# Moving the value differences of a stick-breaking attention into the projection stage, and tying five groups of splits and scans behind others, in a hybrid block on one Trainium2 core

## The chip, the cores and the metric

The kernel runs on one core of one Trainium2 chip. The metric is the device time of one execution in microseconds; lower is better. The times of the kernel before are 2502.95, 2505.12 and 2508.58 us, so the median is 2505.12 us. The profile shown comes from one further execution of the same program.

Engines are named as in the profile: PE (TensorE, matmuls and transposes), PEld (its weight loads), ACT (ScalarE), DVE (VectorE), POOL (GpSimd) and SP (SyncE, which issues the transfers).

## What is computed

One layer of a decoder trunk on 1024 positions of width 1024, all in float32. The part that the change touches is the first sub-layer, token mixing:

```
h = rms_norm(x)
q, k, v, z, xbc, dt_raw, ga, gs = split(h @ w_in)
o_att = stick_breaking_attention(q, k, v)          # 16 heads of 64
o_ssm = ssd_branch(z, xbc, dt_raw, ...)            # Mamba-2, 32 heads in 4 groups
merged = sigmoid(ga) * (o_att @ w_br_att) + sigmoid(gs) * (o_ssm @ w_br_ssm)
x = x + rms_norm(merged @ w_mix_out)
...                                                # then cross-attention and SwiGLU

# one attention head, query t, key s < t:
#   beta[t,s] = sigmoid(q_t . k_s / 8)
#   A[t,s]    = beta[t,s] * prod_{s<j<t} (1 - beta[t,j]),   o_t = sum_s A[t,s] v_s
```

The kernel does not form A. With n[t,j] = sigmoid(-q_t . k_j / 8) = 1 - beta[t,j] and the suffix product N[t,s] = prod_{s<=j<t} n[t,j], A[t,s] = N[t,s+1] - N[t,s]. Summed by parts, the output is a sum of N[t,s] - 1 times the difference of two neighbouring rows of v. These differences, one tile of 128 x 8 x 64 per head, are the "differences of values" of the change.

## The kernel before

Every float32 operand of a matmul is split into a rounded high part and a low part that holds the rest, and a product is three matmuls (high by high, low by high, high by low). `hi_sb` (L110 on) makes a high part, on ACT (L119) or POOL (L115); `lo_of` (L121) makes the low part, by default on DVE (L122). Names that end in h or "hi" are high parts, in l or "lo" low parts.

The stages that matter here, in order of time:

- **First stage, to about 58 us:** norm of x, its transposes in split form, the first products for v.
- **Second stage, about 58 to 270 us:** `rest_of_v` (L494 on) forms the remaining values as five products t1, t2, b22, t3, t4, and stores rows of v to `v_d`; `token_major` (L591 on) forms z in the same way, twice, with seven products each (b11, t2, b21, t1, t3, b22, t4). A `product` (L477) makes four pairs of splits zh and zl (L482, L483: from zr or other tiles, five buffers of each), one for each of four k, and then runs 48 matmuls (L490 to L492); the splits of the next product run beside the matmuls of the present one. In `rest_of_v` the operands t3 and t4 are read back from `tc_d` in eight loads of 256 KB (zk) and split as well (L512, L513).
- **Convolutions and gates, about 270 to 645 us.**
- **Attention, about 645 to 1086 us:** heads in eight pairs. For a pair of heads, projections of q and k are made from loaded weights (wraw, split into whi and wlo) by matmuls mm (L125 to L127). `ev_q` copies the result to qs (ACT, L852 and L853), forms its low part gt (DVE, L854), and moves halves with transfers (L845); `ev_k` does the same for kh and kl (L861 to L863). `scores` (L896) makes for a head and a block b of 128 queries the scores sc (L908, L909), their sigmoid n (ACT, L910) and its suffix product by a scan on DVE (L911) of (b + 1) x 128 elements a row: block 6 has 896, blocks 0 to 3 belong to half 0 of a head and 4 to 7 to half 1. `values` (L916) transposes N by blocks of 128 keys (tr, L925), splits N - 1 into wth (ACT, L928) and wtl (DVE, L929), and sums av with two matmuls per key block (L937, L938), three steps behind the transposes. The last three key blocks of a half are 384, 256 and 128 wide. `interleave` (L955) puts the value steps of one half, the scores of the next half and the projections of the pair after next into one order.
- Before, `differences` (L881) runs in attention: at each even head it loads two shifted copies va and vb of two heads' values from `v_d` (512 KB each, one buffer each), POOL subtracts them (L888, 128x1024), and for each head POOL makes the high and the low part of v (L115, L122).
- **SSD stage from 1086 us:** `open_four` (L1088) loads cfm, btm and others for four chunks and splits them into ch, cl, bh and bl; before, nothing ties these splits to the attention stage. A table load for the exponential is tied behind the last sigmoid of the scores (L990, L996, L997), while the last gates' sigmoids (L875) come later and are not counted in it.

The order on each engine is set by a scheduler at build time from the written order, the dependences and estimated times; each engine then executes its instructions strictly in that order, and SP issues its transfers in order too, so that a transfer that waits for its buffer holds up those behind it. `behind` (L217) adds a tie: the instructions made inside it are put after the named ones on their engine.

## Time and profile before

| | |
|---|---|
| median of 3 runs | 2505.12 us |
| the profiled execution | 2511.1 us, of which the span is 2509.4 us |
| mean granted clock of PE | 0.995 |
| second stage | 58 to 270 us |
| attention | 645 to 1086 us, eight pairs at some 50 us each |
| length of one product of the second stage | 10.9 us (48 matmuls) |

How to read the rows in the prediction. A row of a time line has the start in us, the duration in us (of a run of like instructions when "x4" stands at its end, first start to last end), the engine, the line, the operation, its output and inputs by the program's names, and in brackets how long the engine stood idle just before it and what released it. A row of the list of waits has the engine and what waited, what it waited for, and then the total, the number of times and the longest. A row of the windows has the stretch and its length, then the busy time of PE, PEld, DVE, ACT and POOL with the number of instructions that started in it, the granted clock of PE, the busy share of the transfer engines and GB/s. A row of a group has the count after "x", and behind the bar the busy time in us, the mean of one in ns, and the idle time before.

### The profile page before, as it was taken

What the parts mean: (1) busy time and instruction counts of PE and PEld (TensorE: products, weight loads), DVE (VectorE), ACT (ScalarE), POOL (GpSimd) and SP (SyncE); (2) the same over time, 40 slices, a digit from 0 to 9 for tenths busy, and PEclk for the clock granted to TensorE, in tenths of its full rate; (3) what the DMA queues carried; (4) which work ended last, traced back from release to release, by engine and by line L of the source; (5) the groups of instructions that cost most, each with busy time, mean ns of one, the idle gap of its engine ahead of it and who ended that gap; (6) DMA issues with size and microseconds to landing.
All of it is one profiled execution on the core that took longest, in us unless ns stands there. A gap on an engine that the chain in (4) does not pass through costs nothing. (4 is left out here: it accounts for less than half of the span.)

```text
span 2509.4 us, 33330 instructions
## 1 busy us (share of the span) xinstructions
PE 2447.4 (98%) x12306; PEld 2015.2 (80%) x12306; DVE 1806.5 (72%) x2237; ACT 1165.5 (46%) x2058; POOL 657.3 (26%) x545
## 2 busy tenths in 40 slices
PE   7999999999999999989999999999999999999998
PEld 5788888888778888877877778888888888888887
DVE  7665877776587888689898774487468655666997
ACT  5333455555465666466644312344435333344433
POOL 3221545443211111134444141102012332220001
PEclk9999999999999999999999999999999999999999
DMA  7431443333534343366332481331241322334322
GB/s 249 157 118 47 141 139 113 104 106 93 156 101 110 89 122 89 89 191 207 108 110 77 129 275 59 120 116 51 84 151 63 103 79 76 95 97 164 131 101 101
DMA packets 249132, 295.62 MB, mean 118 GB/s; under 512 B 17023, under 2 KB 169096, under 8 KB 248842
## 3 DMA queue, kind: packets, MB, share of 16 engines
q1 hardware_dynamic: 248682, 292.45, 37.0%
q8 instruction: 97, 1.59, 0.3%
q10 hardware_dynamic: 288, 1.05, 0.1%
q14 instruction: 65, 0.53, 0.1%
HBM read 202.20 MB, written 74.45 MB: 110 GB/s over the span
## 5 line engine op out<-in xcount | busy, mean ns | idle before, releaser
L911 DVE TENSOR_TENSOR_SCAN n<-n,mask 128x128 f32<-128x128 f32 (+7 forms) x128 | 190.0, 1511 | 24.5 <-ACT n L910 21.2
L122 DVE TENSOR_TENSOR sw<-sf,sw 128x512 fp32r<-128x512 f32 x142 | 126.9, 897 | 72.0 <-ACT sw L119 69.9
L119 ACT ACTIVATE sw<-sf 128x512 fp32r<-128x512 f32 x142 | 88.9, 628 | 155.8 <-PE mm L230 139.1
L928 ACT ACTIVATE wth<-tr,mone 128x512 fp32r<-128x512 f32 x192 | 110.7, 585 | 83.3 <-PE tr L925 81.3
L929 DVE SCALAR_TENSOR_TENSOR wtl<-tr,wth 128x512 fp32r<-128x512 f32 x192 | 99.7, 544 | 48.3 <-ACT wth L928 48.3
L693 DVE SCALAR_TENSOR_TENSOR b<-b,prmT,b 128x1023 f32<-128x1023 f32 (+2 forms) x72 | 109.6, 1522 | 16.9 <-ACT b L687 16.3
L122 DVE TENSOR_TENSOR sw<-wr,sw 128x512 fp32r<-128x512 f32 x107 | 99.2, 929 | 23.9 <-ACT sw L119 23.8
L196 POOL TENSOR_TENSOR sf<-wr,wr 128x512 f32<-128x512 f32 x36 | 53.2, 1477 | 229.8 <-DMA wr<-in_w_gu_dram 82.3
L229 PE MATMUL mm<-h,sw 128*128 128x512 f32 x288 | 112.0, 389 | 0.0
L230 PE MATMUL mm<-h,sw 128*128 128x512 f32 x288 | 111.7, 389 | 0.0
L910 ACT ACTIVATE n<-sc 128x512 f32<-128x512 f32 (+1 forms) x192 | 88.6, 494 | 46.6 <-PE tr L925 28.7
L228 PE MATMUL mm<-h,sw 128*128 128x512 f32 x288 | 109.9, 389 | 0.0
L125 PE MATMUL mm<-oth,bw 128*128 128x512 f32 x256 | 104.5, 408 | 3.9 <-DVE a L1259 2.3
L173 POOL TENSOR_SCALAR rstd<-ms 128x1 f32<-128x1 f32 x74 | 26.9, 363 | 307.8 <-ACT x L180 228.3
L127 PE MATMUL mm<-oth,bw 128*128 128x512 f32 x256 | 101.3, 396 | 0.0
L126 PE MATMUL mm<-otl,bw 128*128 128x512 f32 x256 | 101.1, 395 | 0.0
L127 PE MATMUL p<-bw,h 128*128 128x512 f32 x256 | 100.1, 392 | 0.5 <-DVE h L122 0.5
L126 PE MATMUL p<-bw,h 128*128 128x512 f32 x256 | 99.9, 390 | 0.0
L125 PE MATMUL p<-bw,h 128*128 128x512 f32 x256 | 99.7, 390 | 0.0
L925 PE MATMUL tr<-ident,n 128*128 128x128 f32 x576 | 95.4, 274 | 4.0 <-DVE wtl L929 4.0
L115 POOL TENSOR_SCALAR v<-va 128x512 fp32r<-128x512 f32 x16 | 20.6, 1289 | 286.8 <-PE av L938 165.9
L119 ACT ACTIVATE zh<-zr 128x512 fp32r<-128x512 f32 x72 | 45.0, 631 | 104.7 <-PE ma L492 52.3
(664 smaller groups left out, 7753.9 us busy)
## 6 DMA issues: line engine op xcount, KB each, us to landing
wr<-in_w_in_dram SPq DMA_DIRECT2D x36, 512.0 KB
wr<-in_w_gu_dram SPq DMA_DIRECT2D x72, 256.0 KB
zr<-in_w_in_dram SPq DMA_DIRECT2D x28, 512.0 KB
wraw<-in_w_in_dram SPq DMA_DIRECT2D x20, 512.0 KB
gu_d<-t SPq DMA_DIRECT2D x36, 256.0 KB
zs_d<-zo SPq DMA_DIRECT2D x32, 256.0 KB
xs_d<-b SPq DMA_DIRECT2D x32, 256.0 KB
kl<-gt SPq DMA_DIRECT2D x64, 128.0 KB
```

The costliest lines, as they stand in the source:

```text
L119: A.activation(o, i, AF.Copy)
L122: eng.tensor_tensor(o, i, hi.bitcast(F32), ALU.subtract)
L125: first = T.matmul(ps, sh, mh, start=start, stop=False)
L126: T.matmul(ps, sh, ml, start=False, stop=False)
L127: T.matmul(ps, sl, mh, start=False, stop=stop)
L228: T.matmul(ps, w[0][:, k, :], bh, start=first and k == 0, stop=False, skip_group_check=True)
L229: T.matmul(ps, w[0][:, k, :], bl, start=False, stop=False, skip_group_check=True)
L230: ins = T.matmul(ps, w[1][:, k, :], bh, start=False, stop=last and k == 3, skip_group_check=True)
L693: V.scalar_tensor_tensor(acc[:, sh:], y[:, :S - sh], cw(3 - sh, f), acc[:, sh:], ALU.mult, ALU.add)
L911: V.tensor_tensor_scan(nt[:, 0:L][:, ::-1], nt[:, 0:L][:, ::-1], mask[:, S - L:][:, ::-1], 1.0, ALU.mult, ALU.max)
L928: A.activation(wh[:, t0 * P:], pt[:, t0 * P:], AF.Identity, bias=mone)
L929: V.scalar_tensor_tensor(wl[:, t0 * P:], pt[:, t0 * P:], -1.0, wh[:, t0 * P:].bitcast(F32), ALU.add, ALU.subtract)
```

## The change

Five things are changed.

1. In `rest_of_v` the high parts of t3 and t4 are tied behind the last high part of product t2, and the low parts behind its last low part.
2. The differences of values are made in `token_major`: `value_pair` loads va and vb for a pair of heads, `differences` subtracts them on DVE behind the last low part of a product, splits the result on ACT and DVE and stores both heads' tiles to a new scratch `dv_d`. Eight products of the fourteen carry one pair each. In attention, `values_of` only loads a head's finished tile (512 KB, 4 KB a row).
3. The scan of block 6 is tied behind the 256-wide low part of half 0 of the same head.
4. The tie of the exponential's table load (now L1025) covers the gates' sigmoids.
5. `open_four`'s high parts are tied behind the last wth of attention and its low parts behind the last wtl.

The diff, cut:

```diff
                 pa_ = bank("ma")
+                for e in (V, A):
+                    e.on = True
                 product(pa_, a11, "t2", True, True)
+                lasts = [e.last for e in (A, V)]
...
                         nc.sync.dma_start(t, src[:, k, :])
-                        hi_sb(hb[nm][0][:, k, :], t, "a")
-                        lo_of(hb[nm][1][:, k, :], t, hb[nm][0][:, k, :])
+                        with behind(lasts[:1]):
+                            hi_sb(hb[nm][0][:, k, :], t, "a")
+                        with behind(lasts[1:]):
+                            lo_of(hb[nm][1][:, k, :], t, hb[nm][0][:, k, :])
...
+            def value_pair(hp):
+                va, vb = [mk(dvp, [P, NCH, P], F32, n) for n in ("va", "vb")]
+                for t, r in ((va, 0), (vb, 1)):
+                    nc.sync.dma_start(t, v_d[r:S + r, hp * P:(hp + 1) * P].rearrange("(c p) d -> p c d", p=P))
+                loaded.append((hp, va, vb))
+
+            def differences(after):
+                hp, va, vb = loaded.pop()
+                with behind([after]):
+                    V.tensor_tensor(va, va, vb, ALU.subtract)
+                for j in range(2):
+                    dv = va[:, :, j * HD:(j + 1) * HD]
+                    vt = mk(dvp, [P, NCH, P], F32R, "v", 2)
+                    hi_sb(vt[:, :, 0:HD], dv, "a")
+                    lo_of(vt[:, :, HD:P], dv, vt[:, :, 0:HD])
+                    nc.sync.dma_start(dv_d[2 * hp + j], vt.bitcast(F32).rearrange("p c d -> p (c d)"))
+                if hp + 1 < NH // 2:
+                    value_pair(hp + 1)
...
-                product(pa_, a12, "b21", False, True)
+                low = product(pa_, a12, "b21", False, True)
+                if not loaded and j == 1:
+                    value_pair(0)
+                else:
+                    differences(low)
...
-                product(pb_, s1, "t1", True, False)
+                differences(product(pb_, s1, "t1", True, False))
...
-                product(pa_, s3, "t3", True, False)
+                differences(product(pa_, s3, "t3", True, False))
...
+                if loaded:
+                    differences(low)
...
-                    A.activation(gt, ps, AF.Sigmoid)
+                    sig.append(A.activation(gt, ps, AF.Sigmoid))
...
-            def differences(h):
-
-                j = h % 2
-                if j == 0:
-                    va, vb = [mk(vp, [P, NCH, P], F32, n, bufs=1) for n in ("va", "vb")]
...
-                    G.tensor_tensor(va, va, vb, ALU.subtract)
-                    dvs[0] = va
...
-                hi_sb(vt[:, :, 0:HD], dv, "p")
-                lo_of(vt[:, :, HD:P], dv, vt[:, :, 0:HD], G)
-                heads[h]["v"] = vt
+            def values_of(h):
+
+                vt = heads[h]["v"] = mk(vp, [P, NCH, P], F32R, "v")
+                nc.sync.dma_start(vt.bitcast(F32).rearrange("p c d -> p (c d)"), dv_d[h])
...
-                    V.tensor_tensor_scan(nt[:, 0:L][:, ::-1], nt[:, 0:L][:, ::-1], mask[:, S - L:][:, ::-1], 1.0, ALU.mult, ALU.max)
+                    with behind([lows[h, 0, 2]] if b == 6 else []):
+                        V.tensor_tensor_scan(nt[:, 0:L][:, ::-1], nt[:, 0:L][:, ::-1], mask[:, S - L:][:, ::-1], 1.0, ALU.mult, ALU.max)
...
-            sig_last = sig[-1:]
+            sig_last, high_last, low_last = sig[-1:], highs[-1:], [lows[NH - 1, 1, 2 * 4 - 1]]
...
-            hi_sb(bh, btm, "a")
-            lo_of(bl, btm, bh)
...
-            hi_sb(ch, cfm, "a")
-            lo_of(cl, cfm, ch)
+            with behind(high_last):
+                hi_sb(bh, btm, "a")
+                hi_sb(ch, cfm, "a")
+            with behind(low_last):
+                lo_of(bl, btm, bh)
+                lo_of(cl, cfm, ch)
```

In the rows of order that follow, a row has the line, the operation, output and inputs with their buffer numbers, and the shape. Line numbers of the changed kernel differ from those of the kernel before.

**ACT in `rest_of_v`**, around 72 us of the profile. zh are the splits of product t2 (source zr), t3h and t4h those of the operands that are read back. Before:

```order
L119 ACTIVATE t3h_649<-zk_830 128x512
L119 ACTIVATE t4h_651<-zk_834 128x512
L119 ACTIVATE t4h_651<-zk_838 128x512
L119 ACTIVATE t4h_651<-zk_842 128x512
L119 ACTIVATE zh_756<-zr_629 128x512
L119 ACTIVATE zh_760<-zr_631 128x512
```

And in the changed kernel:

```order
L49 ACTIVATE zh_760<-zr_630 128x512
L49 ACTIVATE zh_764<-zr_632 128x512
L49 ACTIVATE zh_768<-zr_632 128x512
L120 ACTIVATE t3h_650<-zk_822 128x512
L120 ACTIVATE t3h_650<-zk_826 128x512
```

The three splits of t2's product now stand ahead of all eight of t3 and t4; before, the first of them stood behind seven.

**DVE in an odd head of attention**, around 696 us of the profile. A row with "mask" is a scan and its last number is the length; wtl are low parts of the weights N - 1. Before:

```order
L929 SCALAR_TENSOR_TENSOR wtl_5711<-tr_5706,wth_5710 128x384
L911 SCALAR_TENSOR_TENSOR n_987_5809<-n_987_5809,mask_5276 128x768
L911 SCALAR_TENSOR_TENSOR n_993_5829<-n_993_5829,mask_5276 128x896
L929 SCALAR_TENSOR_TENSOR wtl_5723<-tr_5719,wth_5722 128x256
L929 SCALAR_TENSOR_TENSOR wtl_5737<-tr_5734,wth_5736 128x128
L911 SCALAR_TENSOR_TENSOR n_1000_5854<-n_1000_5854,mask_5276 128x1024
```

And in the changed kernel, from the same low part on:

```order
L939 SCALAR_TENSOR_TENSOR n_1017_5911<-n_1017_5911,mask_5385 128x768
L957 SCALAR_TENSOR_TENSOR wtl_5825<-tr_5821,wth_5824 128x256
L957 SCALAR_TENSOR_TENSOR wtl_5839<-tr_5836,wth_5838 128x128
L939 SCALAR_TENSOR_TENSOR n_1030_5956<-n_1030_5956,mask_5385 128x1024
L939 SCALAR_TENSOR_TENSOR n_1042_6012<-n_1042_6012,mask_5385 128x128
L957 SCALAR_TENSOR_TENSOR wtl_5887<-tr_5881,wth_5886 128x512
L957 SCALAR_TENSOR_TENSOR wtl_5908<-tr_5903,wth_5907 128x384
L123 TENSOR_TENSOR wlo_6264<-wraw_6261,whi_6263 128x1024
L902 TENSOR_TENSOR gt_5985<-mm_5877,kh_5857 128x512
L939 SCALAR_TENSOR_TENSOR n_1051_6040<-n_1051_6040,mask_5385 128x256
L939 SCALAR_TENSOR_TENSOR n_1060_6075<-n_1060_6075,mask_5385 128x384
L957 SCALAR_TENSOR_TENSOR wtl_5928<-tr_5924,wth_5927 128x256
L939 SCALAR_TENSOR_TENSOR n_1023_5931<-n_1023_5931,mask_5385 128x896
```

The 896-wide scan has left its place ahead of the 256-wide low part (wtl_5723 before, wtl_5825 now) and stands behind the next 256-wide one, eleven instructions later. On PE the transposes of its tile follow: in odd heads three matmuls mm, in even heads six, now stand between the transposes of blocks 4 and 5 and that of block 6, which before followed one another.

**ACT at the start of attention**, around 646 us of the profile. b are copies of the last convolution's transposes, qs those of the first projection of q. Before:

```order
L681 ACTIVATE b_861_5215<-tr_5210 128x512
L852 ACTIVATE qs_5312<-mm_5287 128x512
L853 ACTIVATE qs_5313<-mm_5287 64x512
L119 ACTIVATE whi_5433<-wraw_5431 128x1024
L852 ACTIVATE qs_5312<-mm_5320 128x512
```

And in the changed kernel:

```order
L720 ACTIVATE b_893_5324<-tr_5319 128x512
L120 ACTIVATE whi_5542<-wraw_5540 128x1024
L891 ACTIVATE qs_5421<-mm_5396 128x512
L892 ACTIVATE qs_5422<-mm_5396 64x512
L891 ACTIVATE qs_5421<-mm_5429 128x512
```

The split of the next weights, whi, now stands ahead of both copies of the first half; on DVE wlo likewise stands ahead of gt.

More of the change, by code (lines that the diff above doesn't have):

```diff
@@ L88, in hybrid_block @@
     g_d = scr("g_d", [2 * D, S])
+    dv_d = scr("dv_d", [NH, P, S])
     o_d = [scr(f"o_d{i}", [D, S]) for i in range(2)]
@@ L121, in lo_of @@
     def lo_of(o, i, hi, eng=V):
-        eng.tensor_tensor(o, i, hi.bitcast(F32), ALU.subtract)
+        return eng.tensor_tensor(o, i, hi.bitcast(F32), ALU.subtract)
     def mm3(ps, sh, sl, mh, ml, start, stop):
@@ L456, in hybrid_block @@
             cup = pool(p1, "cumul")
+            dvp = pool(p1, "dv", 1, side="right")
             psp = pool(p1, "psz", 4, PSUM)
@@ L482, in product @@
                     hi_sb(ws[k][0], ts[k // 2][:, k % 2, :], "a")
-                    lo_of(ws[k][1], ts[k // 2][:, k % 2, :], ws[k][0])
+                    low = lo_of(ws[k][1], ts[k // 2][:, k % 2, :], ws[k][0])
                 kc = [(k, c) for k in range(4) for c in range(4)]
@@ L492, in product @@
                     T.matmul(ps[c], bl[:, k, cs], wh, start=False, stop=last and k == 3, skip_group_check=True)
+                return low
             def rest_of_v():
@@ L505, in rest_of_v @@
                 pa_ = bank("ma")
+                for e in (V, A):
+                    e.on = True
                 product(pa_, a11, "t2", True, True)
+                lasts = [e.last for e in (A, V)]
+                for e in (V, A):
+                    e.on, e.last = False, None
                 both(lambda q: V.tensor_tensor(a12[q], a12[q], a11[q], ALU.subtract))
@@ L534, in rest_of_v @@
                     store_v(c, 1, u[c])
+            def value_pair(hp):
[15 more added lines that the diff above has]
+                    value_pair(hp + 1)
+            loaded = []
             def dt_chain(load):
@@ L629, in token_major @@
                     V.tensor_tensor(w[c], u[c], pb_[c], ALU.add)
-                product(pb_, s4, "b22", False, True)
+                low = product(pb_, s4, "b22", False, True)
+                if loaded:
+                    differences(low)
                 for c in range(4):
@@ L633, in token_major @@
                     put(c + 4, i0 + 1, w[c])
-                product(pa_, a22, "t4", False, True)
+                low = product(pa_, a22, "t4", False, True)
+                if loaded:
+                    differences(low)
                 for c in range(4):
@@ L802, in hybrid_block @@
             G.affine_select(mask[:, S - P:], mask[:, S - P:], [[-1, P]], ALU.is_gt, 1.0, base=0, channel_multiplier=1)
-            marks, sig = [], []
+            marks, sig, highs, lows = [], [], [], {}
             PIN = 8
@@ L874, in ev @@
                     gt = mk(t2, [P, HALF], F32, "gt")
-                    A.activation(gt, ps, AF.Sigmoid)
+                    sig.append(A.activation(gt, ps, AF.Sigmoid))
                     nc.sync.dma_start(g_d[gi * P:(gi + 1) * P, half * HALF:(half + 1) * HALF], gt)
                 return dense(C_GA + gi * P, ev)
-            dvs = {}
-            def differences(h):
-                j = h % 2
-                if j == 0:
-                    va, vb = [mk(vp, [P, NCH, P], F32, n, bufs=1) for n in ("va", "vb")]
-                    for t, r in ((va, 0), (vb, 1)):
-                        nc.sync.dma_start(t, v_d[r:S + r, h * HD:(h + 2) * HD].rearrange("(c p) d -> p c d", p=P))
-                    G.tensor_tensor(va, va, vb, ALU.subtract)
-                    dvs[0] = va
-                dv = dvs[0][:, :, j * HD:(j + 1) * HD]
-                vt = mk(vp, [P, NCH, P], F32R, "v")
-                hi_sb(vt[:, :, 0:HD], dv, "p")
-                lo_of(vt[:, :, HD:P], dv, vt[:, :, 0:HD], G)
-                heads[h]["v"] = vt
+            def values_of(h):
+                vt = heads[h]["v"] = mk(vp, [P, NCH, P], F32R, "v")
+                nc.sync.dma_start(vt.bitcast(F32).rearrange("p c d -> p (c d)"), dv_d[h])
             def scores(h, half, tb, ns_):
@@ L899, in run @@
                     if half == 0 and tb == 0:
-                        differences(h)
+                        values_of(h)
                     b = half * 4 + tb
@@ L927, in tr @@
                     wl = mk(wt, [P, HALF], F32R, "wtl")
-                    A.activation(wh[:, t0 * P:], pt[:, t0 * P:], AF.Identity, bias=mone)
-                    V.scalar_tensor_tensor(wl[:, t0 * P:], pt[:, t0 * P:], -1.0, wh[:, t0 * P:].bitcast(F32), ALU.add, ALU.subtract)
+                    highs.append(A.activation(wh[:, t0 * P:], pt[:, t0 * P:], AF.Identity, bias=mone))
+                    lows[h, half, i] = V.scalar_tensor_tensor(wl[:, t0 * P:], pt[:, t0 * P:], -1.0, wh[:, t0 * P:].bitcast(F32), ALU.add, ALU.subtract)
                     st[i] = (wh, wl, t0 * P)
```

## The prediction

> **What bounds the kernel now.** The first view is the head of the page:

> ```profile
> span 2509.4 us, 33330 instructions
> PE 2447.4 (98%) x12306; PEld 2015.2 (80%) x12306; DVE 1806.5 (72%) x2237; ACT 1165.5 (46%) x2058; POOL 657.3 (26%) x545
> ```

> TensorE is busy for 2447.4 of 2509.4 us, and the change takes no matmul away. What can be won is TensorE's 62 us of waiting and the time lost where its granted clock is under 1.0. So the second view is the list of TensorE's waits in the attention stage (645 to 1086 us), where four of the change's parts act:

> ```profile
> PE av L938 <- DVE wtl L929: 7.4, 6, 1.2
> PE tr L925 <- DVE wtl L929: 4.0, 9, 0.6
> PE av L937 <- ACT wth L928: 2.7, 1, 2.7
> PE sc L908 <- DMA kh<-kh: 0.9, 1, 0.9
> ```

> The columns are the total in us, the count and the longest. These four rows hold 15.0 us. The third view is time lines around single waits; they follow with the part that they price.

> **Splits of t3 and t4 behind the last split of t2's product** (second stage). TensorE, ScalarE (ACT) and the granted clock:

> ```profile
> 75.36 1.92 PE L490 MATMUL ma<-zh,t2h 128*128 128x512 f32 x4 [2.89 <-ACT zh L119]
> ...
> 72.22 0.63 ACT L119 ACTIVATE t3h<-zk 128x512 fp32r<-128x512 f32 x1 [3.80 <-DMA zk<-tc_d]
> 72.88 1.92 ACT L119 ACTIVATE t4h<-zk 128x512 fp32r<-128x512 f32 x3
> 74.70 1.13 ACT L119 ACTIVATE zh<-zr 128x512 fp32r<-128x512 f32 x2
> ...
> 75.00:78.00 3.00, 2.63 (x7) 2.05 (x8) 3.00 (x6) 2.92 (x6) 0.00 (x0) 0.60 0.17 23
> 78.00:81.00 3.00, 3.00 (x13) 2.44 (x12) 1.46 (x3) 0.63 (x1) 0.00 (x0) 0.84 0.83 262
> ```

> ACT stood 3.80 us for zk's landing with the running product's zh queued behind it; TensorE then waited 2.89 us. In the new order zh comes first, and ACT was free for it from 68.4 (72.22 - 3.80), so the wait goes whole; the low parts follow on VectorE (DVE). Behind it the clock (the column after POOL's) was 0.60 and 0.84, which loses 3 x 0.40 + 3 x 0.16 = 1.7 us. Together **-4.6** (-2.9 if another gap brings the low clock back). Late next: the eight splits of t3 and t4 now end about 77.9 (72.22 + 9 x 0.63), and the next product's zh after them; it starts near 80.5, a margin of some 2 us.

> **Differences in the second stage instead of on GpSimd (POOL) in attention.** Added per pair of heads: a subtraction of 128x1024, two low and two high parts of 128x512 per partition row, two loads and two stores of 512 KB. The nearest rows:

> ```profile
> 703.92 1.23 DVE L122 TENSOR_TENSOR wlo<-wraw,whi 128x1024 fp32r<-128x1024 f32 x1 [0.85 <-POOL whi L115]
> ...
> L122 DVE TENSOR_TENSOR zl<-zr,zh 128x512 fp32r<-128x512 f32 x10 | 10.7, 1082 | 1.5 <-ACT zh L119 1.5
> ...
> L122 DVE TENSOR_TENSOR zl<-zr,zh 128x512 fp32r<-128x512 f32 x21 | 15.9, 758 | 21.1 <-ACT zh L119 21.1
> ...
> 177.00:203.00 26.00, 26.00 (x116) 21.52 (x116) 22.43 (x26) 10.37 (x18) 15.49 (x6) 1.00 0.30 105
> 203.00:250.00 47.00, 47.00 (x209) 38.92 (x208) 22.29 (x33) 16.70 (x28) 4.80 (x2) 1.00 0.07 24
> ...
> 186.99 2.30 DVE L122 TENSOR_TENSOR zl<-zr,zh 128x512 fp32r<-128x512 f32 x1
> ...
> 194.49 0.39 PE L490 MATMUL ma<-zh,b11h 128*128 128x512 f32 x1
> ```

> So 1.23 + 2 x 0.76 = 2.75 us of DVE and 2 x 0.63 us of ACT per pair, 22 and 10 us in all, under a TensorE that is busy for 26.00 of 26.00 and 47.00 of 47.00 us. From 203 to 250 DVE has 24.7 us free and takes four pairs (11 us). From 177 to 203 it has 3.6 us free beside POOL's sums, where a split lasts 1082 ns (the x10 row) rather than 758 (x21, from 203 to 270). Two pairs fall there: 5.5 us, or 7.8 at that slower pace, so the lows come 2 to 4 us later. The tightest of them ends at 189.29 and is needed at 194.49, which leaves 5.2 us: cost **0**. If the cover fails, up to +5 (a rival, below). The 24 transfers share DMA queues that are 0.30 and 0.07 busy; they stand among zr's loads on SP, which wait for buffers in any case: 0.

> What the move takes away in attention:

> ```profile
> 731.67 2.39 POOL L888 TENSOR_TENSOR va<-va,vb 128x1024 f32<-128x1024 f32 x1 [3.90 <-DMA va<-v_d]
> L115 POOL TENSOR_SCALAR v<-va 128x512 fp32r<-128x512 f32 x16 | 20.6, 1289 | 286.8 <-PE av L938 165.9
> ...
> 731.99 3.15 DVE L911 TENSOR_TENSOR_SCAN n<-n,mask 128x512 f32<-128x512 f32 x1
> 707.06 1.23 DVE L911 TENSOR_TENSOR_SCAN n<-n,mask 128x512 f32<-128x512 f32 x1
> ...
> 656.38 0.37 SPq L887 DMA_DIRECT2D vb<-v_d  x1
> 661.77 0.67 PE L908 MATMUL sc<-kh,qs 128*128 128x128 f32 x3 [0.85 <-DMA kh<-kh]
> ```

> The same scan lasted 3.15 us beside POOL's subtraction and 1.23 us away from it, so the subtraction costs DVE 1.9 us once per pair; that gain is booked with the scan below, where it meets a cost. The load of vb stood ahead of the moves of kh and kl on SP until POOL released its buffer, and TensorE waited 0.85 us for kh; the new load of a finished value waits for no engine's work there: **-0.85** (0 if kh is late for its own sake).

> **Scan of block 6 behind the 256-wide low part.** DVE and TensorE in an odd head, before:

> ```profile
> 695.57 2.00 DVE L911 TENSOR_TENSOR_SCAN n<-n,mask 128x896 f32<-128x896 f32 x1
> 697.49 0.60 DVE L929 SCALAR_TENSOR_TENSOR wtl<-tr,wth 128x256 fp32r<-128x256 f32 x2
> 697.94 0.39 PE L938 MATMUL av<-wtl,v 128*128 128x256 f32 x1 [1.22 <-DVE wtl L929]
> ```

> The 2.00 us scan stands ahead of the low part for which TensorE waits 1.22 us, six times: the 7.4 us of the list. The change puts the scan some 11 us later, behind wlo, gt and two scans of the next block. What is late next is the transpose of the moved scan's tile. Stepping the new DVE order through with the durations of before: whi ends about 703.65, wlo 704.8, gt 705.4, the scans of 256 and 384 at 706.9, the low part at 707.2, scan 896 at 709.1; TensorE reaches the transpose about 708.4. So some 0.7 us (0 to 1.2) of wait come back: a net of about -0.6 per odd head. In even heads the shorter 512-wide scan (-1.9) pays for the added 896-wide one (+2.0) at the same place; of the 4.0 us of tr waits most should go, since TensorE has six projection matmuls ahead of that transpose now: -3. Odd heads give 7 x -0.6 = -4. Together **-7**, between 0 and -11.4 (all of both waits).

> **Start of attention.** Here the new order of ACT is adverse:

> ```profile
> 644.99 0.61 ACT L852 ACTIVATE qs<-mm 128x512 fp32r<-128x512 f32 x1
> 646.28 1.06 ACT L119 ACTIVATE whi<-wraw 128x1024 fp32r<-128x1024 f32 x1
> 647.36 0.60 ACT L852 ACTIVATE qs<-mm 128x512 fp32r<-128x512 f32 x1
> 646.98 0.50 PE L125 MATMUL mm<-b11h,whi 128*128 128x512 f32 x1 [0.51 <-DVE gt L854]
> ```

> whi can start no earlier than 646.28, when the matmuls have left its buffer; it now stands ahead of both qs, which before were done at 646.20. qs end 1.2 us after whi, about 648.5, gt at 649.2 instead of 646.9: **+2.25**, and TensorE's whole wait becomes about 2.8 us. Two waits of this length here (2.89 above, 2.67 below) were followed by the low clock, at 1.7 us each; at 0.7 that adds +1.2. Sum **+3.4**, between 0 (the engine's real order differs) and +4.

> [...]

> **End of attention.** Gates' table and the next stage's parts behind the last head:

> ```profile
> 1063.62 1.28 ACT L997 ACT_TABLE_LOAD   x1
> 1066.67 1.28 ACT L875 ACT_TABLE_LOAD   x1
> 1083.14 0.63 ACT L119 ACTIVATE ch<-cfm 128x512 fp32r<-128x512 f32 x1 [3.20 <-DMA cfm<-cf_d]
> ...
> 1084.30 0.44 PE L937 MATMUL av<-wth,v 128*128 128x384 f32 x1 [2.67 <-ACT wth L928]
> 1091.92 0.49 PE L1137 MATMUL dec<-colrows,keyrows 128*128 128x512 f32 x1 [0.96 <-ACT s L1138]
> ...
> 1086.00:1088.00 2.00, 1.88 (x9) 1.70 (x10) 0.28 (x2) 1.16 (x2) 0.00 (x0) 0.50 0.28 82
> 1088.00:1090.00 2.00, 2.00 (x12) 1.78 (x10) 1.58 (x2) 1.98 (x5) 0.39 (x1) 0.67 0.95 304
> ```

> Before, ACT stood 3.20 us for cfm with the last head's wth behind it, and TensorE waited 2.67 us. In the new order the wth come first. The one table load that is left stands ahead of the last five wth; by my stepping it lets the 384-wide one end near 1081.5 instead of 1084.2: -2.5. The load that held s (0.96) is gone: -1.0. The low clock of 0.50 and 0.67 costs 2 x 0.50 + 2 x 0.33 = 1.7, and has no cause left: -1.5. Together **-5**, between -1 (table load and landing of cfm take the wait over) and -7.

> **Stages behind.** In the stage from 1086 the order around the moved bh and ch changes a little on four engines. TensorE's waits there are single ones, as

> ```profile
> PE dec L1112 <- ACT s L1138: 1.5, 1, 1.5
> ```

> One of them with its 1.7 us of low clock can come or go: 0, between -3 and +3.

> **Sum:** -4.6 + 0 - 0.85 - 7 + 3.4 - 5 + 0 = -14 us. The profiled execution took 2511.1 us (its span and 1.7 us around it), 6 us over the median of 2505.1; the difference is taken as the same for both: 2505.1 - 14 = **2491 us**. A measurement of this kernel tells about 0.2%, 5 us, from no change.

> **Rivals.**
> (1) Slower: the differences delay the second stage. Each subtraction is tied behind a product's last low part, and DVE works in order; if va or vb lands late (POOL stood 3.90 us for va above, and here the loads share SP with zo's stores), or if POOL's sums hold DVE longer, the next zl waits too. It decides where the delay passes the 5.2 us above. At six of the eight products a delay of 8 us would leave a wait of about 3 us each with 1.7 of clock: +28 - 14 = +14, some 2519. For it: DVE's 22.43 of 26. Against it: POOL has 15.49 us in that stretch alone and lead elsewhere is 8 to 9 us. Chance 0.10.
> [...]
> (2) The moved scan returns the attention gain: a new wait of 1.2 us at its transpose in each odd head and nothing won in even ones leaves 0 of the -7: -14 + 7 = -7, some 2498. For it: wlo, gt and three scans now stand close together on DVE, and the stepping leaves them no idle time. Chance 0.22.
> (3) The change does little of what it says: the ties bring the waits only elsewhere (start +4, end -1, scan 0, second stage -2.9): about 2505. Chance 0.12.
> The forecast, 2479 to 2497, has 0.56.

> **Numbers.** The terms' ends add to about -27 and +8 if all fall one way; taken as independent, 2491 -12/+11. To hold eight in ten it takes in rival (2): 2478 to 2503. Faster by over 0.2%, below 2500: 0.56 + most of (2) = 0.75; within 0.2%: 0.13; slower: 0.12.

> **What would show it.** Right: TensorE without idle between 60 and 270 us and a clock of 1.00 from 75 to 81; no wait at av for the 256-wide low part, and waits of under 1 us at the transpose of the 896-wide scan's tile; scans of 512 at 1.2 us throughout; a new wait near 2.8 us at the first b11 matmul after the last conv; one table load near 1080 and no 2.7 us wait for wth. Wrong: waits at ma or mb for zl between 120 and 270; waits of over 1.2 us in each head; a low clock in new places after 1086.

## The result and the profile after

The changed kernel takes 2501.88 us (median of 19 runs, 2499.01 to 2505.54), the kernel before 2508.11 us beside it (19 runs, 2502.95 to 2510.43). The ratio is 0.9978 with a 95% interval of 0.9972 to 0.9984: 6.2 us faster, where 14 were forecast. A later measurement of the same two gave 2502.09 and 2508.99 us, ratio 0.9973 (0.9965 to 0.9982). The median before that the forecast started from, of three runs, was 3 us too low.

The first profiled execution of the changed kernel is shorter than that of before by 10.9 us:

```profile
span 2498.5 us, 33391 instructions
PE 2438.4 (98%) x12306; PEld 2010.1 (80%) x12306; DVE 1807.4 (72%) x2261; ACT 1167.0 (47%) x2072; POOL 604.5 (24%) x505
```

Both programs have 12306 matmuls and transposes, so the start of the n-th one can be compared. The table shows by how much it starts earlier (-) or later (+) than before, for the two profiled executions of the changed kernel (the second is the run e12 below).

| place | n | before, us | first | second |
|---|---|---|---|---|
| after t2's wait | 300 | 87.85 | -4.9 | -5.0 |
| within the second token product | 1000 | 246.62 | -5.0 | -3.0 |
| convolutions begun | 1200 | 293.53 | -3.9 | -1.9 |
| ahead of attention | 2820 | 644.14 | -4.3 | -2.2 |
| first b11 in attention | 2840 | 649.42 | -2.0 | +1.4 |
| behind kh's wait | 2900 | 663.62 | -3.2 | +0.3 |
| near the end of attention | 4950 | 1055.41 | -8.1 | -4.8 |
| SSD stage begun | 5300 | 1116.38 | -6.7 | -3.7 |
| end | 12300 | 2499.56 | -11.0 | -8.3 |

Read from top to bottom, the steps are these. **t3 and t4:** the windows of the changed kernel show TensorE busy throughout and a clock of 1.00 where before there was 0.60:

```profile
72.00:75.00 3.00, 3.00 (x15) 2.50 (x14) 3.00 (x6) 2.91 (x5) 0.00 (x0) 1.00 0.91 344
75.00:78.00 3.00, 3.00 (x15) 2.49 (x14) 2.13 (x4) 1.36 (x4) 0.00 (x0) 1.00 0.20 40
```

**Second stage and the change to the convolutions:** two costs that were forecast at nothing. First the low parts of the second token product's b11, in the kernel before and in the changed one, then the change at 270 us in the changed one:

```profile
191.02 1.28 DVE L122 TENSOR_TENSOR zl<-zr,zh 128x512 fp32r<-128x512 f32 x2
197.21 0.39 PE L490 MATMUL ma<-zh,b11h 128*128 128x512 f32 x1
...
191.48 1.28 DVE L123 TENSOR_TENSOR zl<-zr,zh 128x512 fp32r<-128x512 f32 x2
192.22 0.39 PE L492 MATMUL ma<-zh,b11h 128*128 128x512 f32 x1
...
264.89 1.71 DVE L123 TENSOR_TENSOR sw<-sf,sw 128x512 fp32r<-128x512 f32 x1 [0.39 <-ACT sw L120]
268.82 0.68 DVE L679 TENSOR_TENSOR zk<-zk,ma 128x512 f32<-128x512 f32 x1
269.64 0.47 PE L229 MATMUL mm<-t1h,sw 128*128 128x512 f32 x1 [1.10 <-DVE zk L679]
```

In the changed kernel the first of the two low parts is ready at 192.2, at the very moment when its slice of the product begins (192.22); before, it was ready at 191.7 for a slice that began at 197.21, a lead of 5.5 us. In the second execution of the changed kernel TensorE waited for it:

```profile
194.22 0.50 PE L493 MATMUL ma<-zl,b11h 128*128 128x512 f32 x1 [1.69 <-DVE zl L123]
```

At 270 us the additions (zk) that free TensorE's next accumulators stand on DVE behind a low part (sw) of the first convolution's weights. What SP issued some 20 us earlier, without the pairs of differences (first row, run e1 below; TensorE is within 0.3 us of the same position) and in the changed kernel (the other three):

```profile
248.52 6.85 SPq L193 DMA_DIRECT2D wr<-in_w_in_dram  x3
...
248.64 0.92 SPq L561 DMA_DIRECT2D dv_d<-v  x2
249.85 2.16 SPq L473 DMA_DIRECT2D zs_d<-zo  x3
252.10 3.09 SPq L194 DMA_DIRECT2D wr<-in_w_in_dram  x3
```

The first load of weights (wr) is issued 3.6 us later, behind the stores of the last differences, which wait for DVE's low parts, and the stores of zo that follow them.

**Start of attention:** the wait that was forecast is there, to 0.02 us:

```profile
642.03 1.06 ACT L120 ACTIVATE whi<-wraw 128x1024 fp32r<-128x1024 f32 x1 [1.18 <-PE mm L127]
645.00 0.50 PE L126 MATMUL mm<-b11h,whi 128*128 128x512 f32 x1 [2.78 <-DVE gt L893]
```

**Attention:** TensorE's list of waits from 640 to 1066 us has lost the 1.2 us waits for the low part, and has two new kinds, here at its head:

```profile
PE av L965 <- ACT oT L969: 4.5, 6, 0.7
PE tr L953 <- DVE n L939: 4.4, 8, 0.6
```

The time line of an odd head (first three rows) and of an even head shows where they come from:

```profile
703.19 2.01 DVE L939 TENSOR_TENSOR_SCAN n<-n,mask 128x896 f32<-128x896 f32 x1
705.30 1.21 DVE L939 TENSOR_TENSOR_SCAN n<-n,mask 128x512 f32<-128x512 f32 x1
705.26 0.44 PE L953 MATMUL tr<-ident,n 128*128 128x128 f32 x2 [0.54 <-DVE n L939]
...
730.31 0.26 DVE L957 SCALAR_TENSOR_TENSOR wtl<-tr,wth 128x128 fp32r<-128x128 f32 x1
731.11 0.38 PE L953 MATMUL tr<-ident,n 128*128 128x128 f32 x2
731.25 0.31 PE L966 MATMUL av<-wtl,v 128*128 128x128 f32 x1
731.39 0.62 PE L953 MATMUL tr<-ident,n 128*128 128x128 f32 x4
731.53 0.69 ACT L956 ACTIVATE wth<-tr,mone 128x512 fp32r<-128x512 f32 x1 [3.70 <-PE tr L953]
732.12 0.59 ACT L969 ACTIVATE oT<-av 128x512 f32<-128x512 f32 x1
732.76 0.50 PE L965 MATMUL av<-wth,v 128*128 128x512 f32 x1 [0.74 <-ACT oT L969]
```

In odd heads the transpose waits for the scan that was moved. In even heads the low part is ready in time: it ends at 730.57, and the last product of the half (731.25) starts 0.7 us later without a wait. What has moved is the order of TensorE and ACT. The transposes of the moved scan's tile (731.11) now stand behind six projection matmuls, so the split wth that is made from them starts at 731.53 and stands on ACT ahead of oT, the copy that empties the accumulator av. The next half's first product waits for oT, and only four transposes are left in between to fill the time. The same place without the tie (run e2 below), where this wth runs earlier, oT follows its product at once and eight transposes cover it:

```profile
729.99 0.69 ACT L956 ACTIVATE wth<-tr,mone 128x512 fp32r<-128x512 f32 x1 [2.33 <-PE tr L953]
731.22 1.04 PE L953 MATMUL tr<-ident,n 128*128 128x128 f32 x8
731.41 0.60 ACT L969 ACTIVATE oT<-av 128x512 f32<-128x512 f32 x1 [0.74 <-PE av L966]
732.07 0.50 PE L965 MATMUL av<-wth,v 128*128 128x512 f32 x1
```

The 512-wide scan takes 1.21 us where it took 3.15.

**End of attention:** the wait for wth has shrunk from 2.67 to 0.98 us, and four waits follow at the start of the next stage. From n = 5100 to 5300 TensorE stands idle for 4.2 us, before for 2.0:

```profile
1071.16 1.28 ACT L1025 ACT_TABLE_LOAD   x1
1073.29 0.49 PE L965 MATMUL av<-wth,v 128*128 128x512 f32 x1 [0.98 <-ACT wth L956]
1080.67 1.25 PE L1085 MATMUL mm<-ident,wraw 128*128 128x128 f32 x8 [1.38 <-DVE mlo L1088]
1082.57 0.51 PE L126 MATMUL pst<-s2r,bh 128*128 128x512 f32 x1 [0.65 <-ACT s2r L120]
1085.46 0.51 PE L1167 MATMUL dec<-colrows,keyrows 128*128 128x512 f32 x1 [1.35 <-ACT s L1168]
1086.74 0.38 PE L126 MATMUL mm<-mh,bw 128*128 128x256 f32 x1 [0.78 <-DVE mlo L1088]
...
1088.00:1091.00 3.00, 3.00 (x16) 3.00 (x16) 3.00 (x3) 2.43 (x4) 2.66 (x3) 0.50 0.99 313
```

The last row is a window: behind these waits the clock is 0.50 again, as it was before (0.50 and 0.67 from 1086 to 1090 us).

The last rows of the table hold the clock as well: the profile of before has two stretches of 6.8 us at half clock behind 1178 and 1461 us that the first profile of the changed kernel has not, worth 3.4 us each; the changed one has a stretch of 3.4 us at 1303 us, worth 1.7, that before has not. What went ahead of such stretches comes at the end.

### The profile page after: what moved, and what is told of

The parts are those of the page before. It is cut to its first block, busy times and chain, and to the rows that moved or that the text cites. A ratio compares the mean times of both kernels' runs of the same rounds, so it can differ in the third digit from the quotient of the medians.

```text
span 2498.5 us, 33391 instructions
## 1 busy us (share of the span) xinstructions
PE 2438.4 (98%) x12306; PEld 2010.1 (80%) x12306; DVE 1807.4 (72%) x2261; ACT 1167.0 (47%) x2072; POOL 604.5 (24%) x505
## 5 line engine op out<-in xcount | busy, mean ns | idle before, releaser
L939 DVE TENSOR_TENSOR_SCAN n<-n,mask 128x128 f32<-128x128 f32 (+7 forms) x128 | 170.0, 1350 | 27.7 <-ACT n L937 24.4
L116 POOL TENSOR_SCALAR whi<-wraw 128x1024 fp32r<-128x1024 f32 x13 | 14.8, 1136 | 395.0 <-PE mm L127 366.9
L937 ACT ACTIVATE n<-sc 128x512 f32<-128x512 f32 (+1 forms) x192 | 86.7, 495 | 37.0 <-PE tr L953 20.6
L120 ACT ACTIVATE sw<-wr 128x512 fp32r<-128x512 f32 x107 | 67.1, 628 | 58.3 <-PE mm L231 51.4
```

Source lines behind the costliest of these rows:

```text
L120: A.activation(o, i, AF.Copy)
L939: V.tensor_tensor_scan(nt[:, 0:L][:, ::-1], nt[:, 0:L][:, ::-1], mask[:, S - L:][:, ::-1], 1.0, ALU.mult, ALU.max)
```

## Experiments

All times are medians against runs of the kernel before on the same chip; positions are starts of the n-th matmul against before, as in the table above.

| run | us | ratio to before (95%) |
|---|---|---|
| e1, splits of t3 and t4 alone | 2503.58 | 0.9987 (0.9978 to 0.9997) |
| e2, changed, scan untied | 2502.11 | 0.9975 (0.9966 to 0.9983) |
| e4, changed, end as before | 2504.11 | 0.9991 (0.9983 to 1.0000) |
| e5, changed, differences in attention | 2508.82 | 1.0004 (0.9995 to 1.0013) |
| e6, changed, qs first | 2498.95 | 0.9963 (0.9951 to 0.9975) |
| e7, e6 and pairs earlier | 2498.26 | 0.9966 (0.9954 to 0.9979) |
| e8, e6 and cl later | 2498.72 | 0.9963 (0.9949 to 0.9976) |
| e9, e6 and scan moved one place | 2490.43 | 0.9934 (0.9921 to 0.9946) |
| e10, e9 and additions first | 2491.67 | 0.9935 (0.9922 to 0.9947) |
| e11, e10 and cl later | 2492.51 | 0.9937 (0.9923 to 0.9951) |
| e12, changed, again | 2502.09 | 0.9973 (0.9965 to 0.9982) |
| e13, e9 and no pair at t4 | 2489.80 | 0.9927 (0.9913 to 0.9941) |

### e1: the splits of t3 and t4 alone

The kernel before, and of the diff only the hunks on product t2 and on the loop over `tc_d`.

> The kernel before with one part of the change alone: the splits of t3 and t4 tied behind the last splits of product t2. Theory A (each part acts where the prediction put it, the parts that fell short are others): the wait of 2.9 us at 72 us is gone, TensorE is 3.2 us earlier from there on (4.9 us where the profile of before had its stretch of low clock), and nothing of it is lost at the change to the convolutions at 270 us. Time 3 to 5 us under before. Theory B (being earlier is itself what costs at 270 us, since the next stage's weights do not come earlier): a new wait of about 1.1 us there, time 2 to 4 us under before.

Theory A holds: TensorE is 5.1 us earlier at n = 600 and 5.3 at n = 1200; at 270 us there is no wait for zk. The low parts of the second token product's b11 keep their lead (5.2 and 5.5 us). So neither the wait at 270 us nor the lost lead comes from being earlier.

### e5: all parts but the differences

```diff
-                differences(product(pb_, s1, "t1", True, False))
+                product(pb_, s1, "t1", True, False)
...
-                        values_of(h)
+                        differences(h)
```

`differences` is again that of before, with POOL in attention; `value_pair` and the other four calls are gone.

> The changed kernel with the differences of values made in attention by POOL, as before; the other four parts stay. Theory A (moving the differences costs 1.2 us at 270 us, where the next stage's weights are issued behind the stores of the differences, and gains 1.1 us of kh's wait and about 3 us of DVE time in attention): no wait for zk above 0.3 us at 270 us; the wait of 0.85 us for kh and scans of 3.15 us are back; at the end of attention TensorE is 2 to 4 us later than in the changed kernel. Theory B (POOL's work in attention cost nothing, all the gain is the scan tie's): within 1 us of the changed kernel there or earlier than it.

Theory A, and more of it than expected. No wait for zk at 270 us (-5.0 at n = 1200). In attention the waits are

```profile
PE tr L934 <- DVE wtl L938: 6.4, 7, 1.0
PE av L946 <- ACT oT L950: 4.4, 6, 0.7
PE tr L934 <- DVE n L920: 3.8, 7, 0.5
PE sc L916 <- DMA kh<-kh: 1.9, 1, 1.9
```

and TensorE goes from -4.0 behind kh's wait to +3.2 at n = 4950, 11.2 us later than in the changed kernel, some 5 of them in three stretches of low clock. The scans of 3.15 us are back, now with the 896-wide scan ahead of them: with POOL's subtraction in place, the tied scan makes attention longer than before. The four other parts together are worth nothing here, 1.0004. With the differences moved, the same four parts go along with a gain of 6 us; without that, with none.

### e2: the changed kernel without the tie of the scan

```diff
-                    with behind([lows[h, 0, 2]] if b == 6 else []):
+                    if True:
```

> The changed kernel without the tie of the 896-wide scan. Theory A (the tie gives little, most of the attention stage's gain is POOL's lighter load): the waits of 1.2 us for the 256-wide low part come back six times, but the waits of 0.54 us for the scan and of 0.74 us for the copy oT go: attention within 2 us of the changed kernel's. Theory B (the tie is what gains): attention takes 5 to 8 us more than in the changed kernel, time equal to before.

Theory A. The wait for the 256-wide low part is back (7.2 us, six times), those for the scan and for oT are gone. Attention (n = 2900 to 4950) gains 3.8 us over before, against 4.9 with the tie; the time is that of the changed kernel. The tie as it was made is worth about 1 us.

### e9: the scan moved by one place

```diff
-                    with behind([lows[h, 0, 2]] if b == 6 else []):
+                    with behind([lows[h - 1, 1, 6]] if b == 6 and h else []):
```

On top of e6. The low part for which TensorE waited belongs to the head before (key block 6 of its second half).

> The changed kernel with qs first, and with the 896-wide scan tied behind the 256-wide low part of the head before (the one that TensorE waited for) instead of the next one, so that it moves by one place and not by twelve. Theory A (the tie moved the scan too far: the gain at the low part comes back as the waits of 0.54 us at the scan's transpose and of 0.74 us for oT): neither the 1.2 us waits nor these two kinds appear, attention takes 4 to 7 us less than with qs first alone. Theory B (DVE has no room in that stretch, any place of the scan costs TensorE the same): the waits change their place, for the 128-wide low part or the next scan, and attention stays within 2 us.

Theory A. TensorE's waits from 640 to 1062 us, and DVE at the place that the prediction showed:

```profile
PE av L972 <- DVE wtl L963: 1.6, 2, 1.0
PE sc L942 <- DMA kl<-gt: 0.8, 1, 0.8
PE mm L126 <- DVE gt L897: 0.5, 1, 0.5
PE sc L941 <- ACT n L943: 0.5, 1, 0.5
```

```profile
689.46 1.75 DVE L945 TENSOR_TENSOR_SCAN n<-n,mask 128x768 f32<-128x768 f32 x1
691.12 0.40 DVE L963 SCALAR_TENSOR_TENSOR wtl<-tr,wth 128x256 fp32r<-128x256 f32 x1
691.44 2.01 DVE L945 TENSOR_TENSOR_SCAN n<-n,mask 128x896 f32<-128x896 f32 x1
693.37 0.27 DVE L963 SCALAR_TENSOR_TENSOR wtl<-tr,wth 128x128 fp32r<-128x128 f32 x1
```

Attention gains 12.7 us over before (n = 2900 to 4950), 7.5 more than e6, and the kernel 7 to 8.5 (by the ratios, 0.9963 to 0.9934, and by the medians). This is the forecast's term and more: DVE had room for the scan behind the one low part that mattered, not eleven places on. Between n = 2900 and 4950 TensorE stood idle for 11.5 us before, 9.2 in the changed kernel and 1.3 here. The rest of the gain, some 2.5 us in both, is busy time of TensorE (380.3 us before, 377.7 and 377.8), which no run takes apart.

### e6: qs first at the start of attention

```diff
-                    A.activation(q1[HD:P], ps[HD:P], AF.Copy)
-                    V.tensor_tensor(low, ps, q0.bitcast(F32), ALU.subtract)
+                    hi1 = A.activation(q1[HD:P], ps[HD:P], AF.Copy)
+                    lo1 = V.tensor_tensor(low, ps, q0.bitcast(F32), ALU.subtract)
+                    if hp == 0 and half == 0:
+                        first_q.extend((hi1, lo1))
...
-        hi_sb(hi, raw, eng)
-        lo_of(lo, raw, hi)
+        with behind(late[:1]):
+            hi_sb(hi, raw, eng)
+        with behind(late[1:]):
+            lo_of(lo, raw, hi)
```

`late` is `first_q` for the weights of the second pair's q and empty for all others.

> The changed kernel with one more tie: at the start of attention the high part of the third weights is tied behind the first projection's copies qs, and its low part behind gt. Theory A (the order of ACT there is what costs 1.8 us): the wait of 2.8 us at the first b11 matmul shrinks to 0.5 us or less and every later matmul is 2.2 us earlier; 2 us faster than the changed kernel, more where the long wait brings the low clock. Theory B (the wait only moves: whi is then late for the projection that uses it): within 0.5 us of the changed kernel, with a new wait at the matmuls of that projection.

Theory A: the wait for gt is 0.5 us, the position stays at -3.6 where the changed kernel falls from -4.3 to -2.0, and no new wait appears. 3 us faster than the changed kernel by the medians; the intervals of the ratios overlap a little.

### e4: the end of attention as before

The two hunks on `open_four` and on `sig.append` of the gates are undone.

> The changed kernel with the end of attention as before: the gates' sigmoids are not counted in the tie of the table load, and the next stage's parts bh, bl, ch, cl are tied to nothing. Theory A (the tail's gain is handed back in the next stage: bh, ch, bl and cl run behind the last head and delay what the first chunks wait for): the wait of 2.7 us for wth comes back at the end of attention, the waits of 1.4, 0.7, 1.4 and 0.8 us within 10 us behind it go, and TensorE stands within 1.5 us of the changed kernel at the 5300th matmul and later. Time within 2 us of the changed kernel. Theory B (the tail gains and something else took it): 3 to 5 us slower than the changed kernel.

Between the two. The wait for wth is back (2.43 us), of the four behind it the two for mlo are gone, while those for s (1.8 us in two) and s2r (0.7 and 0.3) stay, and from n = 4950 to 5300 TensorE loses 1.0 us against before, where the changed kernel loses 1.3: at this place the ties won nothing, as theory A says. But the kernel is 2 us slower than the changed one, with intervals that touch. Between the two profiles the difference of 3.7 us is almost all clock (13.7 us at half clock here, in stretches at 643, 1080 and 1090 us, against 6.8); whether the median's 2 us are more than that, a gain of the ties further behind, stays open.

### e8: cl behind the memory's low parts

```diff
-                lo_of(cl, cfm, ch)
+            with behind(mlows[1:2]):
+                lo_of(cl, cfm, ch)
```

On top of e6; `mlows` collects the low parts mlo of `memory`.

> The changed kernel with qs first, and with the low part cl of the first four chunks tied behind the second low part mlo of the memory instead of standing ahead of it on DVE. Theory A (the tail's gain is lost because bl and cl hold DVE at the start of the next stage): the wait of 1.4 us for mlo falls to 0.7 us or less and TensorE is 0.7 to 1.5 us earlier at the 5300th matmul than with qs first alone. Theory B (that stage is bound by other things there, loads and ACT): the next wait grows by as much and the 5300th matmul stays within 0.4 us.

Both have a part. The wait for mlo is 0.6 us and TensorE is 1.0 us earlier at the 5300th matmul than e6, measured from n = 4950. But the wait for s2r has grown from 0.8 to 1.3 us, and at n = 5850 the two are level (-1.7 and -1.8 from n = 4950). The time is the same. The positions are blurred by the clock: from n = 4950 to 5300 this profile has 6.8 us at half clock and e6 has 3.4, while TensorE's idle time falls from 7.2 to 5.4 us. So DVE is part of what that stage is short of; what the tie is worth is not shown beyond the equal medians.

### e7: the pairs of differences one product earlier

```diff
-                low = product(pa_, a12, "b21", False, True)
-                if not loaded and j == 1:
-                    value_pair(0)
-                else:
-                    differences(low)
+                if j == 1:
+                    value_pair(0)
+                differences(product(pa_, a12, "b21", False, True))
```

On top of e6.

> The changed kernel with qs first, and with the eight pairs of differences one product earlier (five in the first token product, three in the second), so that the last stores stand well ahead of the next stage's weights on SP. Theory A (those stores in SP's queue are what delays the weights): the wait of 1.1 to 1.7 us for zk at 270 us falls to 0.3 us or less, every later matmul is 1.2 us earlier than with qs first alone. Theory B (the delay comes from being earlier or from ACT's and DVE's own queues): the wait stays within 0.4 us of what it was.

Theory A at its place: at 270 us no wait for zk is left. But the second token product's b11 now waits 2.1 us for zl, so that n = 1200 stands at -2.5 instead of -3.2: what was won at one end was lost at the other. Being later is not what removes the wait at 270 us: the second execution of the changed kernel is as late there (-3.0 at n = 1000) and waits 1.08 us for zk.

### e10 and e11: additions first, and with cl later

```diff
+            with behind(late if i in (1, 2, 4, 5) and not on_pool else ()):
-            lo_of(w[1], t, w[0], G if on_pool else V)
+                lo_of(w[1], t, w[0], G if on_pool else V)
```

In `winograd_weights`; `late` is the last addition (L679 of the changed kernel).

> The kernel with qs first and the scan moved by one place, and in the convolution weights the low parts made of sums (sf) tied behind the last addition of the second stage. Theory A (the wait of about 1 us for zk at 270 us comes from a low part that waits for its late weights ahead of the additions on DVE): that wait falls to 0.3 us or less, and every later matmul is 0.8 to 1.2 us earlier than without the tie. Theory B (the additions are late by DVE's work alone): the wait stays, or goes over to the first sw.

Theory B: the wait for zk is gone, and a wait of 1.4 us for the low part that was put back takes its place at 279 us; n = 1700 is later than in e9 (-2.3 against -3.1).

> As the run before, and cl of the first four chunks behind the second low part mlo of the memory. If the stage behind attention is bound by DVE at its start, the wait for mlo is below 0.7 us and the 5300th matmul is 0.5 to 1.2 us earlier than in the run before; if not, it stays within 0.4 us. In both cases the time is within 2 us of that run.

The 5300th matmul stands within 0.3 us of e10, the time within 1 us. Here too the clock stands in between: e11 has 6.8 us at half clock from n = 4950 to 5300 and 6.0 us of idle time, e10 none and 7.9. At 270 us one wait took the place of the other; at 1080 us the gain in waits did not show in the time.

### e13: no pair at the first token product's t4

```diff
-                low = product(pa_, a22, "t4", False, True)
-                if loaded:
-                    differences(low)
+                product(pa_, a22, "t4", False, True)
```

On top of e9, with e7's edit, so that the pairs stand at b21, t1, t3 and b22 of both token products.

> The kernel with qs first and the scan moved by one place, and with the pair of differences behind the first token product's t4 moved to that token product's b21, so that no subtraction falls between 177 and 203 us, where POOL's sums slow DVE. Theory A (the pair at t4 is what used up the 5 us of lead that the low parts of the second token product had): the low parts of its b11 are ready 3 us or more ahead of their matmuls, as in the kernel before, and no wait for zl appears; 0.5 to 2 us faster than without this edit. Theory B (any added pair in the second stage eats the same lead): a wait for zl of 1 us or more appears at b11 or at the first token product's own products, and the time is the same or worse.

Half of theory A: no wait for zl, and TensorE keeps its -5.2 until 270 us. But the lead of the second low part of b11 is 0.6 us, not 3, so the pair at t4 was not the cause. The time lines of POOL and SP show a cause further back. POOL's first sum for that product starts at 172.59 us in e1 (DVE and SP without the pairs, otherwise the same position) and at 175.64 in the changed kernel; the loads of its operands zr, which SP issues at 150.20 and 161.08 in e1, are issued at 153.16 and 163.10, behind stores of differences that wait for DVE and the load of va that follows them. In e13 POOL's sums, later still, run beside DVE's additions zo, which took 0.63 us each in e1 (first row) and take 1.65 here:

```profile
184.12 1.88 DVE L470 TENSOR_TENSOR zo<-zk,zo 128x512 f32<-128x512 f32 x3
...
183.38 2.86 POOL L637 TENSOR_TENSOR zr<-zr,zr 128x1024 f32<-128x1024 f32 x1
184.18 6.62 DVE L474 TENSOR_TENSOR zo<-zk,zo 128x512 f32<-128x512 f32 x4 [0.21 <-ACT zo L473]
```

That SP order was not changed by itself; the link from there to the lead is argued from these rows. Time 2489.80 us, the fastest of all, within the interval of e9.

### e12: the changed kernel again, and the low clock

> The changed kernel once more, for a second profile of it. Theory A (the low clock follows a window of the 3.413 us grid in which TensorE stood idle for over about 1.75 us, wherever the grid happens to lie): the wait of 2.8 us at the start of attention is there again, and the low clock follows it exactly if over 1.75 us of it lie in one window; waits of 2.2 us and more elsewhere likewise. Theory B (the low clock depends on the length of the wait alone): it never follows the 2.8 us wait, as in the first profile. Time within 0.1% of the first measurement.

Theory A. The wait at the first b11 is 2.78 us in both profiles of the changed kernel (and in e4). In the first, no low clock follows; here it does:

```profile
646.00:649.00 3.00, 1.92 (x5) 1.53 (x6) 1.72 (x3) 1.45 (x3) 0.00 (x0) 0.60 0.42 94
649.00:652.00 3.00, 3.00 (x13) 2.42 (x12) 0.00 (x0) 0.00 (x0) 0.00 (x0) 0.83 0.82 256
```

In each trace the stretches of low clock begin at multiples of 3.413 us from each other (in before at 75.57 and 1085.92 us, 1010.35 us or 296 times 3.4133 us apart; in the first profile of the changed kernel at 1087.62 and 1302.66 us, 215.04 us or 63 times), and 3.413 us is their length or half of it, but for the one at the program's end. Cut into such windows, the wait lies in the first profile as 1.67 and 1.11 us in two windows, here with 2.30 us in one. The same 2.78 us stand in e2 as 1.20 and 1.58 us, without a low clock, and in e4 with 2.06 us in one window, followed by it.

## Why the prediction was half right

The direction and most mechanisms were right; the size was not, by 8 us. Term by term, against the first profile and the experiments:

- **t3 and t4, -4.6:** right. From n = 250 (71.41 us before) to n = 300, all thirteen profiles with this part gain 4.7 to 4.8 us.
- **Differences in the second stage, 0:** wrong in two places. The step "they stand among zr's loads on SP, which wait for buffers in any case: 0" failed: the stores wait for DVE and hold SP, and the loads behind them come later (by 3.6 us in the rows of SP above; there are 32 transfers, not 24). At 270 us that costs 1.1 us (e1, e5 and e7 without it, the other runs with the pairs 0.9 to 1.7; e10 and e11 trade it for another wait). The step "the lows come 2 to 4 us later" failed too: beside e1, where TensorE is at the same place, the low part of b11's second slice came 5.6 us later in the first execution and 7.6 in the second, which then waits 1.7 us. Rival (1) named this mechanism, at a price of 28 us that did not come.
- **kh's wait, -0.85:** right, -1.1 from n = 2840 to 2900.
- **Attention, -7:** -4.9 (n = 2900 to 4950). The step of the odd heads came close: a new wait of 0.7 was stepped out, 0.54 was measured. The step of the even heads, "most should go, since TensorE has six projection matmuls ahead of that transpose now: -3", failed: the waits for tr went, and a wait of 0.74 us for oT came in six of them. The same six matmuls hold back the split wth, which then stands ahead of oT on ACT; the prediction had followed DVE and TensorE there, but not ACT. e2, without the tie, gains 3.8 us, so the tie itself is worth 1 us as it was made; e9 gains 12.7 with the scan one place on. Rival (2) had the direction, for 2 of its 7 us.
- **Start of attention, +3.4:** +2.25 was right (+2.2 at n = 2840 against n = 2820), and e6 takes it away. The 1.2 us for the clock were 0 in one profile and some 1.4 in the other.
- **End of attention, -5:** the step that failed most, by some 6 us in the first profile: up to the last weights of the last head the gain came (-1.3 at n = 5085, and -2.8 at n = 5100), but from n = 4950 to 5300 the changed kernel loses 1.3 us. Of its three parts, the wait for wth shrank by 1.7 us where 2.5 were forecast. For s, "the load that held s (0.96) is gone: -1.0": the table load is gone, but the wait for s is 1.35 us. For the clock, "has no cause left: -1.5": half clock came again, at 1088 us in the first profile and at 1090 in the second, behind 2.03 and 1.78 us of idle time within one window of the grid described below. What the forecast left out is where the moved work stands now: bh and ch on ACT and bl and cl on DVE run at the very start of the next stage, where TensorE waits for just these engines (s2r and s on ACT, mlo on DVE). e4, without the ties, loses 1.0 us there, with twice the time at half clock. By the whole kernel's time the ties are worth 2 us (e4), with intervals that touch.
- **Sum:** with -5, +1.2 at 270 us, +2.2, -1.1 and -4.9, TensorE is some 8 us earlier at the end of attention, as the table says, and the next stage gives 1 to 2 back. The medians' 6.2 us fit that. The 10.9 us between the two first profiles hold the clock besides: 20 us of before's profile ran at half clock outside its last 5 us (10 us lost), against 7 us of the changed one's (3 lost).

The price of a wait in clock needs a word, since the prediction took it from the length of two waits (2.89 and 2.67 us). Over all 14 traces of this study, cut into windows of 3.413 us on the grid of each trace's own stretches, TensorE stood idle for 1.75 us or more in 27 windows (outside the program's first 35 us and its end, and without windows that were at half clock already), and all 27 were followed by half clock. Three of them lie in the profile of before (2.89 us of idle time in the window from 72.16 us, 2.13 us from 1082.50 and 1.89 us from 1457.97) and two in the first of the changed kernel (2.03 us from 1084.21 and 2.30 us from 1299.25). Of 19 windows with 1.5 to 1.75 us of idle time 6 were followed by half clock (in before the one with 1.55 us from 1174.66, but not the one with 1.71 us from 1133.70), of 59 with 1.15 to 1.5 us none. So in these traces 1.75 us, about half of one window, was enough each time, and whether a wait of 2 to 3 us cost another 1.7 us (3.413 us at half clock) went with where the grid lay in that execution.

## What to carry to other kernels

Tie a late instruction behind the one that it disturbed, and not further: each place more puts it, or what follows from it, ahead of something else that is waited for, and what waits there may be two steps and two engines away (here the transposes of the moved scan's tile, the split made from them, the copy behind that split that empties an accumulator). Work that is moved out of a wait has to be followed to where it stands next; at a stage's start it stands in front of the same engines. When work moves to a stage with idle engines, the queue that issues its transfers is the resource to check: a store that waits for its data delays the loads behind it (here by 2 to 3.6 us).
